# A two-layer decoder step on one core: first projection tiles, last LayerNorm and attention scores rearranged

## The chip, the cores and the metric

The kernel runs on one core of a Trainium2 chip. The core has a matrix engine (PE, with its weight loads shown apart as PEld), a vector engine (DVE), a scalar engine (ACT), a third elementwise engine (POOL), and a queue engine (SP) that mostly issues DMAs. The metric is the device time of one execution in microseconds (us), as the median of the runs; a profiled execution also has a span, from its first to its last instruction.

## The reference

One step of a trunk with two layers over 256 prompt positions, 16 learned meta tokens ahead of them, and 8 samples of 8 tokens: 336 token columns of width 2048, all in fp32.

```
layer 0 (HGRN2):  h = x @ w_in  (2048 x 8192), split into q, f, i, g
                  gated linear recurrence per head (16 heads of 128 x 128 state), RMS norm, * silu(g)
                  y = o @ w_out;  x = LayerNorm(alpha * x + y)
layer 1 (GQA):    h = x @ w_in  (2048 x 4608), split into q (32 heads of 64), k, v (4 kv heads of 64), g
                  s = (q . k) / 8 inside a window of 128;  sink softmax;  o = p @ v;  o * silu(g)
                  y = o @ w_out;  x = LayerNorm(alpha * x + y) -> y_prompt, y_sample
```

Outputs are also the new recurrent states and the new key and value caches. Prompt queries see keys of the previous and of their own block; sample queries see 128 cached keys and the 8 new ones.

## The kernel before, in words

Tokens stand along the columns (the free axis), features along the 128 partitions: `xh[k]`, `xl[k]` for k = 0..15 hold the input as a high and a low part in fp32r (a rounded float32 which PE takes in one pass, where a plain fp32 matmul shows two records). `trans_x(k)` (L297) makes them: four PE transposes (two prompt blocks, 64 sample rows, 16 meta rows) into one PSUM tile, one ACT copy for the high part and one DVE subtract for the low part.

A **projection tile** is 128 output features against all token columns. `Stream.run` (L185) walks a list `seq` of pairs (tile, kc), kc being a quarter of the 2048 contraction rows; a pair is four steps, one per k, and a step is three matmuls (L212 low weight x high input, L213 high x low, L214 high x high). Weights come by DMA (`raw`, L140, 14 pairs ahead), ACT rounds them (`conv_hi`, L150) and DVE subtracts (`conv`, L161). With `kouter` several tiles go through the quarters in step. After each step `st.step()` lets up to two side chains emit their next piece; a chain's `yield n` is n steps. So the order in each engine's queue is fixed while the program is built, and each engine takes its queue in order. PSUM tiles come from three pools: `pj` (3), `lv` (2), `mm` (3).

**The start** (L750-775): the first tile of f, of q and of i go in step and g0 follows alone; SP issues f0's first weights and then the input. The first four `trans_x` stand ahead of or at the first step, the other twelve in the chain `prologue` (L357), one every few steps. Seven warm-up matmuls (L314) come first of all.

**Attention** (L1018-1150): `prompt_chain(j)` takes a q tile of two heads on 64 rows each. The keys `kzh`, `kzl` have two column groups per kv head with zeros in the other head's rows, so that one matmul over 128 rows gives both heads' scores: three matmuls of 2x144 columns and three of 2x256. `sample_chain(q, u)` does likewise in plain fp32 with `kzs` and `knz`: one matmul of 128 columns and four of 256 on column quarters. `zeros()` writes the zeros.

**The end**: for each output tile j `epi_y(j)` (L1208) adds the residual, transposes (L1227), takes `bn_stats` and multiplies by the LayerNorm gain `yg`. `open_y()` (L1193), which allocates the buffers and loads `yg`, is called when the first output tile is finished. After the last tile `stats()` merges sixteen statistics, makes 1/std on POOL and a small matrix; `final_norm()` (L1303) makes the nine remaining 128x512 correction tiles on PE, adds each to the scaled value on DVE (L1319) and sends it out from SP.

Of the kernel before, what the change touches and what calls it, by code (L numbers as in the profile page):

```python
# [110 lines left out]
class Stream:  # L111
# [77 lines left out]
    def run(self):  # L189
        e = self.e  # L190
        nc = e.nc
        while self.i < len(self.seq):
            t, kc = self.seq[self.i]
            if t.get("before"):
                t["before"](kc)
            self.raw(self.i + e.DR)
            self.conv_hi(min(self.i + e.DC + 1, self.nc + 2))
            if "ps" not in t:
                t["ps"] = e.pj.tile([P, 512], F32, tag="pj", name=f"pj_{t['name']}")
                t["done"] = 0  # L200
            n0, n = t["t0"], t["n"]
            ps = t["ps"][:, :n]
            while ("hl", kc) not in t:
                self.conv(self.nc + 1)
            hi, lo = t.pop(("hl", kc))
            for kk in range(KC):
                k = kc * KC + kk
                xh = t["xh"][k][:, n0:n0 + n]
                xl = t["xl"][k][:, n0:n0 + n]
                t["done"] += 1  # L210
                first, last = t["done"] == 1, t["done"] == KT
                nc.tensor.matmul(ps, lo[:, kk, :], xh, start=first, stop=False)  # L212
                nc.tensor.matmul(ps, hi[:, kk, :], xl, start=False, stop=False)  # L213
                nc.tensor.matmul(ps, hi[:, kk, :], xh, start=False, stop=last)  # L214
# [12 lines left out]
def hybrid_trunk(tc, x_prompt, x_sample, state_hgrn, cache_k, cache_v, meta, w_in0, lb_logits, norm_w, w_out0,  # L227
# [7 lines left out]
    with es:  # L235
# [45 lines left out]
        wst = xes.enter_context(tc.tile_pool(name="wst", bufs=8, side="right"))  # L281
# [15 lines left out]
        def trans_x(k):  # L297
            t = xc[k]
            ps = pm(f"xT{k}")
            nc.tensor.transpose(ps[:, 16:144], t[:, 0, :], ident)  # L300
            nc.tensor.transpose(ps[:, 144:272], t[:, 1, :], ident)
            nc.tensor.transpose(ps[:, 272:336], t[0:64, 2, :], ident[0:64, 0:64])
            nc.tensor.transpose(ps[:, 0:16], t[64:80, 2, :], ident[64:80, 64:80])
            split(xh[k][:, 0:T], xl[k][:, 0:T], ps[:, :T])

        warm = ct("warm", [P, 1])
        nc.scalar.activation(warm, ones[:, 0:1], AF.Exp)
# [5 lines left out]
        for _ in range(7):  # L313
            nc.tensor.matmul(pw[:, 0:128], ones, ones, start=True, stop=True)  # L314
# [436 lines left out]
        first = [tiles[nm, 0] for nm in "fqi"]  # L751
# [4 lines left out]
        st.add([tiles["g", 0]] + [tiles[nm, h] for h in range(1, H) for nm in "fqig"])  # L756
        st.raw(1)
        load_x(0, 2)
        load_x(2, 2)
        st.raw(2)  # L760
        load_x(4, 4)
        st.raw(3)
        st.raw(6)
        load_x(8, 4)
        st.raw(8)
        load_x(12, 4)
        st.conv(1)
        for k in range(2):
            trans_x(k)
        started = []  # L770

        def before(kc):
            if not started:
                started.append(1)
                for k in range(2, KC):
                    trans_x(k)
                st.spawn(prologue())
# [107 lines left out]
        def open_l1():  # L885
# [7 lines left out]
            zero = L["oT"][:, 0, 0:NP]  # L893
            nc.vector.memset(zero, 0.0)
# [6 lines left out]
            for q in range(4):  # L901
                for nm in ("kzh", "kzl"):
                    t = ap1.tile([P, 2, NP], F32R, tag=f"{nm}{q}", name=f"{nm}{q}")
                    L[nm, q] = t
                t = ap1.tile([P, 2, NS], F32, tag=f"knz{q}", name=f"knz{q}")
                nc.gpsimd.memset(t, 0.0)
                L["knz", q] = t
                L["qs", q] = ap1.tile([P, 8, 4, 8], F32, tag=f"qs{q}", name=f"qs{q}")
            for q in range(2):
                t = ap1.tile([P, 4, 2, P], F32, tag=f"kzs{q}", name=f"kzs{q}")  # L910
                nc.gpsimd.memset(t, 0.0)
                L["kzs", q] = t

            def zeros():
                yield 20
                for q in range(4):
                    for nm in ("kzh", "kzl"):
                        nc.scalar.copy(L[nm, q][0:64, 1, :], zero[0:64, :])
                        nc.scalar.copy(L[nm, q][64:128, 0, :], zero[64:128, :])
                        yield 4  # L920
            st.spawn(zeros())

        def epi_k(i):
            def epi(ps):
# [8 lines left out]
                def chain():  # L933
# [8 lines left out]
                    def spread(src, u, half):  # L942
                        q, r = 2 * i + u, slice(64 * half, 64 * half + 64)
                        split(L["kzh", q][r, half, :], L["kzl", q][r, half, :], src[r, 0:NP])
                        nc.gpsimd.tensor_copy(L["knz", q][r, half, :], src[r, NP:T])
# [77 lines left out]
        def prompt_chain(j, pq):  # L1023
# [11 lines left out]
            pa = lv.tile([P, 512], F32, tag="lv", name=f"sa{j}")  # L1035
            pb = lv.tile([P, 512], F32, tag="lv", name=f"sb{j}")
# [8 lines left out]
            for c, (ps, n, m0, o) in enumerate(((pa, 144, 8, 0), (pb, 256, 152, 144))):  # L1045
                nc.vector.scalar_tensor_tensor(sm[:, :, o:o + n], ps[:, 0:2 * n].rearrange("p (h k) -> p h k", h=2),
                                               0.125, cst[:, m0:m0 + n].unsqueeze(1).to_broadcast([P, 2, n]),
                                               op0=ALU.mult, op1=ALU.add)
# [34 lines left out]
        def sample_chain(q, u):  # L1083
# [13 lines left out]
            for half in range(2):  # L1097
                r = slice(64 * half, 64 * half + 64)
                nc.scalar.copy(L["kzs", u][r, :, half, :], pt[r, :].rearrange("p (b k) -> p b k", b=4))
# [4 lines left out]
            ps = lv.tile([P, 512], F32, tag="lv", name=f"ss{q}_{u}")  # L1104
            nc.tensor.matmul(ps[:, 256:384], qs[:, 4 * u:4 * u + 4].rearrange("p b j t -> p (b j t)"), knz,
                             start=True, stop=True, skip_group_check=True)
            for i in range(4):
                b = 4 * u + i
                nc.tensor.matmul(ps[32 * i:32 * i + 32, 0:256], qs[:, b], L["kzs", u][:, i], start=True, stop=True,
                                 tile_position=(0, 32 * i), skip_group_check=True)  # L1110
# [3 lines left out]
            for n, m0, o, src in ((128, 408, 0, 0), (64, 536 + 64 * u, 128, 256)):  # L1114
                nc.vector.scalar_tensor_tensor(
                    sm[:, :, o:o + n], ps[:, src:src + 2 * n].rearrange("p (h k) -> p h k", h=2), 0.125,
                    cst[:, m0:m0 + n].unsqueeze(1).to_broadcast([P, 2, n]), op0=ALU.mult, op1=ALU.add)
# [74 lines left out]

        def open_y():  # L1193
            while L["ngate"] < KT:
                st.step()
# [4 lines left out]
            for nm, shape, dt in (("z", [P, 2, D], F32), ("zs", [P, D // 2], F32), ("bn", [P, 3, KT, 6], F32),  # L1200
# [3 lines left out]
            nc.sync.dma_start(Y["g"], ln_g[1:2, :].to_broadcast([P, D]))  # L1204
# [3 lines left out]
        def epi_y(j):  # L1208
            def epi(ps):
                if j == 0:  # L1210
                    open_y()

                def chain():
# [15 lines left out]
                    for b in range(3):  # L1229
                        nc.vector.bn_stats(Y["bn"][:, b, j, :], pt[:, 128 * b:128 * b + 128])  # L1230
# [41 lines left out]
        def stats():  # L1272
            M, S = Y["M"], Y["S"]
            mv = Y["p2"].tile([P, 3, 2], F32, tag="mv", name="mv", bufs=1)
            for b in range(3):
                nc.vector.bn_aggr(mv[:, b, :], Y["bn"][:, b].rearrange("p c s -> p (c s)"))
# [26 lines left out]
        def final_norm():  # L1303
# [3 lines left out]
            todo = [(0, 1), (0, 2), (2, 0), (1, 0), (1, 1), (2, 1), (0, 3), (1, 2), (1, 3)]  # L1307
            pools = [(e.pj, "pj"), (e.pj, "pj"), (lv, "lv"), (lv, "lv"), (mm, "mm"), (e.pj, "pj"), (mm, "mm"),
                     (mm, "mm"), (e.pj, "pj")]
            R = []  # L1310
            for i, (b, c) in enumerate(todo):
# [3 lines left out]
                                 start=True, stop=True, tile_position=(32 * b, 0))  # L1315
            for i, (b, c) in enumerate(todo):
                cs = slice(512 * c, 512 * c + 512)
                zz = Y["z"][:, b, cs] if b < 2 else Y["zs"][:, cs]
                nc.vector.scalar_tensor_tensor(zz, zz, rstd[:, b:b + 1], R[i], op0=ALU.mult, op1=ALU.add)  # L1319
                if b < 2:  # L1320
                    nc.sync.dma_start(y_prompt[0, 128 * b:128 * b + 128, cs], zz)
# [14 lines left out]
        def before_y(kc):  # L1336
            while not gated:
                st.step()
            if "n" not in Y:
                Y["n"] = 0  # L1340
                Y["p1"] = yes.enter_context(tc.tile_pool(name="y1", bufs=4))
                st.spawn(residuals())
            for t in yt:
# [43 lines left out]
```

## Time and profile before

| what | value |
|---|---|
| median of 3 runs | 1191.69 us (1191.45 to 1192.14) |
| profiled execution: own time / span | 1193.07 us / 1191.3 us |
| PE, PEld busy | 1170.4 us (98%), 1125.5 us (94%) |
| DVE, ACT, POOL busy | 792.3, 609.9, 236.8 us (67%, 51%, 20%) |
| DMA | 171.47 MB, mean 144 GB/s |
| granted PE clock over the span | 0.991 |

The span is the time from the first to the last instruction of that execution; its own time is what the run reports for the same execution, 1.77 us more. A PE record begins when the matmul starts and ends when its result is out, so that the records of a dense stream overlap: the distance between two starts is the price of a matmul there, not its duration.

### The profile page before, as it was taken

The numbers are of one execution on the slowest core, as the hardware profiler recorded it, in microseconds if no ns is written. First come the engines' busy times: TensorE is split into PE (matmuls) and PEld (weight loads), VectorE is DVE, ScalarE is ACT, GpSimd is POOL, SyncE is SP. The second block draws the span as 40 slices with busy tenths as digits, with TensorE's granted clock in tenths as the row PEclk, the third lists the DMA queues.
The fourth block names the chain that finished last, engine by engine and source line by source line (L and its number), as shares of the span: only waits on it lengthen the run. The fifth ranks groups of instructions, "written<-read, shape, count | busy, mean of one in ns | idle before, by whom it ended". The sixth has DMA issues, their size and how long they took to land.

```text
span 1191.3 us, 26295 instructions
## 1 busy us (share of the span) xinstructions
PE 1170.4 (98%) x10163; PEld 1125.5 (94%) x10163; DVE 792.3 (67%) x2049; ACT 609.9 (51%) x1779; POOL 236.8 (20%) x350
## 2 busy tenths in 40 slices
PE   9999999999999999999999999999999999999995
PEld 7999999999999999999999999988888899999994
DVE  3765666565666565566578777678777767777675
ACT  4655545545555545555444446666656655553340
POOL 3022212212212212212224332000000011144420
PEclk8999999999999999999999999999999999999997
DMA  9545655445655545655455555634244345555532
GB/s 260 145 128 159 178 146 145 138 134 160 180 145 146 138 133 161 179 145 151 136 146 145 143 146 166 180 103 129 74 116 117 89 126 162 151 151 178 144 93 89
DMA packets 328462, 171.47 MB, mean 144 GB/s; under 512 B 19085, under 2 KB 325613, under 8 KB 328167
## 3 DMA queue, kind: packets, MB, share of 16 engines
q1 hardware_dynamic: 327792, 168.82, 50.2%
q8 instruction: 80, 1.31, 0.5%
q0 software_dynamic: 544, 0.97, 0.2%
q14 instruction: 46, 0.37, 0.1%
HBM read 156.97 MB, written 14.42 MB: 144 GB/s over the span
## 4 chain that ended last, share of the span: by engine, by line
PE 92%; issue 3%; DVE 2%; DMA 1%; ACT 1%; POOL 1%; SPq 0%; POOLq 0%; DVEq 0%; ACTq 0%
PE pj_q L212 7%; PE pj_g L212 7%; PE pj_g L213 7%; PE pj_g L214 6%; PE pj_q L213 6%; PE pj_q L214 6%; PE pj_f L212 4%; PE pj_i L212 3%; PE pj_i L214 3%; PE pj_i L213 3%; PE pj_f L214 3%; PE pj_f L213 3%; PE pj_z L214 3%; PE pj_z L213 3%; PE pj_z L212 3%
## 5 line engine op out<-in xcount | busy, mean ns | idle before, releaser
L212 PE MATMUL pj_q<-xh,wlo_q 128*128 128x336 f32 (+1 forms) x512 | 166.6, 325 | 0.0
L212 PE MATMUL pj_g<-xh,wlo_g 128*128 128x336 f32 (+1 forms) x512 | 162.9, 318 | 0.0
L213 PE MATMUL pj_q<-xl,whi_q 128*128 128x336 f32 (+1 forms) x512 | 161.2, 315 | 0.0
L214 PE MATMUL pj_q<-xh,whi_q 128*128 128x336 f32 (+1 forms) x512 | 160.9, 314 | 0.0
L213 PE MATMUL pj_g<-xl,whi_g 128*128 128x336 f32 (+1 forms) x512 | 160.6, 314 | 0.0
L214 PE MATMUL pj_g<-xh,whi_g 128*128 128x336 f32 (+1 forms) x512 | 160.4, 313 | 0.0
L212 PEld LDWEIGHTS pj_q<-xh,wlo_q 128*128 128x128 f32 x512 | 97.1, 190 | 5.8 <-issue 4.7
L212 PEld LDWEIGHTS pj_g<-xh,wlo_g 128*128 128x128 f32 x512 | 96.6, 189 | 1.5 <-issue 1.3
L213 PEld LDWEIGHTS pj_q<-xl,whi_q 128*128 128x128 f32 x512 | 97.3, 190 | 0.5
L214 PEld LDWEIGHTS pj_q<-xh,whi_q 128*128 128x128 f32 x512 | 97.1, 190 | 0.0
L213 PEld LDWEIGHTS pj_g<-xl,whi_g 128*128 128x128 f32 x512 | 96.8, 189 | 0.1
L214 PEld LDWEIGHTS pj_g<-xh,whi_g 128*128 128x128 f32 x512 | 96.6, 189 | 0.0
L169 DVE TENSOR_TENSOR wlo_g<-raw_g,whi_g 128x512 fp32r<-128x512 f32 x128 | 90.4, 743 | 0.6 <-ACT whi_g L158 0.6
L169 DVE TENSOR_TENSOR wlo_q<-raw_q,whi_q 128x512 fp32r<-128x512 f32 x128 | 85.1, 684 | 5.3 <-ACT whi_q L158 5.3
L212 PE MATMUL pj_f<-xh,wlo_f 128*128 128x336 f32 x256 | 83.7, 327 | 0.0
L213 PE MATMUL pj_f<-xl,whi_f 128*128 128x336 f32 x256 | 81.5, 318 | 0.0
L214 PE MATMUL pj_f<-xh,whi_f 128*128 128x336 f32 x256 | 81.5, 318 | 0.0
L212 PE MATMUL pj_i<-xh,wlo_i 128*128 128x336 f32 x256 | 81.4, 318 | 0.0
L212 PE MATMUL pj_z<-oh,wlo_z 128*128 128x336 f32 x256 | 81.3, 317 | 0.0
L214 PE MATMUL pj_z<-oh,whi_z 128*128 128x336 f32 x256 | 81.1, 317 | 0.0
L213 PE MATMUL pj_z<-ol,whi_z 128*128 128x336 f32 x256 | 81.0, 316 | 0.0
L213 PE MATMUL pj_i<-xl,whi_i 128*128 128x336 f32 x256 | 80.9, 316 | 0.0
(401 smaller groups left out, 3161.2 us busy)
## 6 DMA issues: line engine op xcount, KB each, us to landing
raw_g<-in_hgrn_w_in_dram SPq DMA_DIRECT2D x32, 512.0 KB
raw_z<-in_hgrn_w_out_dram SPq DMA_DIRECT2D x32, 512.0 KB
raw_q<-in_swa_w_in_dram SPq DMA_DIRECT2D x32, 512.0 KB
raw_g<-in_swa_w_in_dram SPq DMA_DIRECT2D x32, 512.0 KB
raw_y<-in_swa_w_out_dram SPq DMA_DIRECT2D x32, 512.0 KB
raw_f<-in_hgrn_w_in_dram SPq DMA_DIRECT2D x30, 512.0 KB
raw_q<-in_hgrn_w_in_dram SPq DMA_DIRECT2D x30, 512.0 KB
raw_i<-in_hgrn_w_in_dram SPq DMA_DIRECT2D x30, 512.0 KB
```

The costliest lines, as they stand in the source:

```text
L169: e.nc.vector.tensor_tensor(lo, t.pop(("raw", kc)), hi.bitcast(F32), op=ALU.subtract)
L212: nc.tensor.matmul(ps, lo[:, kk, :], xh, start=first, stop=False)
L213: nc.tensor.matmul(ps, hi[:, kk, :], xl, start=False, stop=False)
L214: nc.tensor.matmul(ps, hi[:, kk, :], xh, start=False, stop=last)
```

## The change

Five things are edited.

1. The tiles f0, q0, i0 and g0 go in step (g0 in a bank of the `lv` pool). The first weight DMA is issued by ACT, ahead of ACT's table load; SP begins with the input. Weights and input are asked for in another order, `wst` has nine buffers, and there are eight warm-up matmuls.
2. `trans_x` makes three transposes: sample and meta rows are one block of 80 rows. The parts are now written by two ACT copies and two DVE subtracts, since prompt and sample columns stand in another order in PSUM. Three `trans_x` come ahead of the stream, the fourth after its first step.
3. Prompt scores: each head has its own 64 rows and its own PSUM tile, and twelve matmuls of 144 or 256 columns on row halves (`tile_position=(64 * h, 0)`) take the place of six. The zero halves, and what writes them, are gone. Sample scores: sixteen matmuls on row halves and column quarters take the place of five.
4. `open_y` runs in a chain of its own as soon as all gates are done, and `yg` is loaded in four pieces.
5. Last LayerNorm: fifteen of the sixteen statistics are merged one tile early; the epsilon is folded into them. Of the nine corrections the three for the second prompt block (columns 512 on) are scaled on ACT, copied from PSUM by ACT, added on POOL and sent from ACT's queue; DVE keeps six.

```
 def trans_x(k):
-            nc.tensor.transpose(ps[:, 16:144], t[:, 0, :], ident)
-            nc.tensor.transpose(ps[:, 144:272], t[:, 1, :], ident)
-            nc.tensor.transpose(ps[:, 272:336], t[0:64, 2, :], ident[0:64, 0:64])
-            nc.tensor.transpose(ps[:, 0:16], t[64:80, 2, :], ident[64:80, 64:80])
-            split(xh[k][:, 0:T], xl[k][:, 0:T], ps[:, :T])
+            nc.tensor.transpose(ps[:, 80:208], t[:, 0, :], ident)
+            nc.tensor.transpose(ps[:, 208:336], t[:, 1, :], ident)
+            nc.tensor.transpose(ps[:, 0:80], t[0:80, 2, :], ident[0:80, 0:80])
+            nc.scalar.copy(xh[k][:, 0:NP], ps[:, NS:T])
+            nc.scalar.copy(xh[k][:, NP:T], ps[:, 0:NS])
+            nc.vector.tensor_tensor(xl[k][:, 0:NP], ps[:, NS:T], xh[k][:, 0:NP].bitcast(F32), op=ALU.subtract)
...
 def prologue():
-            yield 2
+            trans_x(3)
+            yield 8
             for k in range(KC, KT):
                 trans_x(k)
-                yield 3
+                yield 2 if k < 2 * KC - 1 else 4
...
-        first = [tiles[nm, 0] for nm in "fqi"]
+        first = [tiles[nm, 0] for nm in "fqig"]
+        first[3]["bank"] = lv, "lv"
...
-        st.raw(1)
+        st.raw(1, nc.scalar)
+        nc.scalar.activation(warm, ones[:, 0:1], AF.Exp)
         load_x(0, 2)
         load_x(2, 2)
-        st.raw(2)
+        st.raw(4)
         load_x(4, 4)
-        st.raw(3)
-        st.raw(6)
+        st.raw(8)
         load_x(8, 4)
-        st.raw(8)
+        st.raw(10)
         load_x(12, 4)
         st.conv(1)
-        for k in range(2):
+        for k in range(3):
             trans_x(k)
...
 def prompt_chain(j, pq):
-            for ps, n, t0, k0, k1 in ((pa, 288, 0, 0, 144), (pb, 512, 128, 16, 272)):
-                o = ps[:, 0:n]
-                nc.tensor.matmul(o, ql[:, t0:t0 + 128], kh[:, :, k0:k1], start=True, stop=False)
-                nc.tensor.matmul(o, qh[:, t0:t0 + 128], kl[:, :, k0:k1], start=False, stop=False)
-                nc.tensor.matmul(o, qh[:, t0:t0 + 128], kh[:, :, k0:k1], start=False, stop=True)
+            for o, n, t0, k0 in ((0, 144, 0, 0), (144, 256, 128, 16)):
+                for i, (a, b) in enumerate(((ql, kh), (qh, kl), (qh, kh))):
+                    for h in range(2):
+                        nc.tensor.matmul(pa[h][:, o:o + n], a[hs[h], t0:t0 + 128], b[hs[h], k0:k0 + n], start=i == 0,
+                                         stop=i == 2, tile_position=(64 * h, 0), skip_group_check=True)
...
 def sample_chain(q, u):
+            for o, n in ((0, 128), (128, 64)):
+                for i in range(4):
+                    for h in range(2):
+                        r = slice(64 * h, 64 * h + 64)
+                        nc.tensor.matmul(ps[h][32 * i:32 * i + 32, o:o + n], qs[r, 4 * u + i],
+                                         knz[r, :] if o else L["kzs", u][r, i], start=True, stop=True,
+                                         tile_position=(64 * h, 32 * i), skip_group_check=True)
...
+        def opening():
+            while L["ngate"] < KT:
+                yield 1
+            open_y()
...
 def stats():
-                nc.vector.bn_aggr(mv[:, b, :], Y["bn"][:, b].rearrange("p c s -> p (c s)"))
+                nc.vector.bn_aggr(mv[:, b, :], Y["ag"][:, b, :])
-            nc.vector.tensor_scalar(rstd, mv[:, :, 1], LN_EPS, None, op0=ALU.add)
-            nc.gpsimd.tensor_tensor(rstd, rstd, mhalf[:, 0:3], op=ALU.pow)
+            nc.gpsimd.tensor_tensor(rstd, mv[:, :, 1], mhalf[:, 0:3], op=ALU.pow)
...
 def final_norm():
-            todo = [(0, 1), (0, 2), (2, 0), (1, 0), (1, 1), (2, 1), (0, 3), (1, 2), (1, 3)]
+            todo = [(0, 1), (1, 1), (2, 0), (0, 2), (1, 2), (2, 1), (0, 3), (1, 3), (1, 0)]
+            for c in range(1, 4):
+                nc.scalar.activation(part(1, c), part(1, c), AF.Copy, scale=rstd[:, 1:2])
...
+                if b == 1 and c:
+                    r = Y["g"][:, 512 * c:512 * c + 512]
+                    nc.scalar.copy(r, R[i])
+                    nc.gpsimd.tensor_tensor(zz, zz, r, op=ALU.add)
+                    late.append((c, zz))
+                    continue
...
+            for c, zz in late:
+                nc.scalar.dma_start(y_prompt[0, 128:256, 512 * c:512 * c + 512], zz)
```

The order of the queues moves at three places that matter below. First, ACT at the start, before (`xh_78` to `xh_81` are the high parts for k = 0 to 3, `whi_q_0` the rounded first weight quarter of q0):

```order
L158 CAST whi_f_0_223<-raw_f_0_187 128x512
L264 CAST xh_78<-xT_227 128x336
L264 CAST xh_79<-xT_234 128x336
L264 CAST xh_80<-xT_243 128x336
L264 CAST xh_81<-xT_250 128x336
L158 CAST whi_q_0_267<-raw_q_0_197 128x512
L158 CAST whi_i_0_269<-raw_i_0_203 128x512
```

And with the change:

```order
L158 CAST whi_f_0_228<-raw_f_0_187 128x512
L305 CAST xh_78<-xT_232 128x272
L306 CAST xh_78<-xT_232 128x64
L305 CAST xh_79<-xT_240 128x272
L306 CAST xh_79<-xT_240 128x64
L305 CAST xh_80<-xT_248 128x272
L306 CAST xh_80<-xT_248 128x64
L158 CAST whi_q_0_266<-raw_q_0_198 128x512
L158 CAST whi_i_0_268<-raw_i_0_200 128x512
L305 CAST xh_81<-xT_274 128x272
L306 CAST xh_81<-xT_274 128x64
```

The input's fourth part now stands behind the first weights of q0 and i0. Second, PE at the scores of the first q tile, before:

```order
L1039 MATMUL sa_10566<-kzh_10074,ql_10547 128x288
L1040 MATMUL sa_10566<-kzl_10075,qh_10546 128x288
L1041 MATMUL sa_10566<-kzh_10074,qh_10546 128x288
L1039 MATMUL sb_10567<-kzh_10074,ql_10547 128x512
L1040 MATMUL sb_10567<-kzl_10075,qh_10546 128x512
L1041 MATMUL sb_10567<-kzh_10074,qh_10546 128x512
```

And with the change (`sa` is now the first head's tile, `sb` the second's):

```order
L1030 MATMUL sa_10564<-kzh_10094,ql_10545 128x144
L1030 MATMUL sb_10565<-kzh_10094,ql_10545 128x144
L1030 MATMUL sa_10564<-kzl_10095,qh_10544 128x144
L1030 MATMUL sb_10565<-kzl_10095,qh_10544 128x144
L1030 MATMUL sa_10564<-kzh_10094,qh_10544 128x144
L1030 MATMUL sb_10565<-kzh_10094,qh_10544 128x144
L1030 MATMUL sa_10564<-kzh_10094,ql_10545 128x256
L1030 MATMUL sb_10565<-kzh_10094,ql_10545 128x256
```

The row halves alternate, and each instruction has half the columns that both heads had together. Third, SP where the gain `yg` is asked for, before (each `raw_y` is half a contraction of an output tile's weights):

```order
L147 DMA raw_y_0_14337<-in_swa_w_out_dram 128x8x128
L147 DMA raw_y_2_14387<-in_swa_w_out_dram 128x8x128
L147 DMA raw_y_0_14431<-in_swa_w_out_dram 128x8x128
L147 DMA raw_y_2_14470<-in_swa_w_out_dram 128x8x128
L147 DMA raw_y_0_14509<-in_swa_w_out_dram 128x8x128
L147 DMA raw_y_2_14547<-in_swa_w_out_dram 128x8x128
L1204 DMA yg<-in_ln_g_dram 128x2048
L1205 DMA yb<-in_ln_b_dram 128x512
```

And with the change:

```order
L147 DMA raw_y_0_14535<-in_swa_w_out_dram 128x8x128
L147 DMA raw_y_2_14585<-in_swa_w_out_dram 128x8x128
L147 DMA raw_y_0_14629<-in_swa_w_out_dram 128x8x128
L1198 DMA yg<-in_ln_g_dram 128x512 x4
L1199 DMA yb<-in_ln_b_dram 128x512
```

Both pieces begin at the fourth output tile's first half, so the gain is asked for three weight loads earlier.

More of the change, by code (lines that the diff above doesn't have):

```diff
@@ L902, in open_l1 @@
                 for nm in ("kzh", "kzl"):
[L903 to L907, printed above, removed]
+                    L[nm, q] = ap1.tile([P, NP], F32R, tag=f"{nm}{q}", name=f"{nm}{q}")
+                L["knz", q] = ap1.tile([P, NS], F32, tag=f"knz{q}", name=f"knz{q}")
                 L["qs", q] = ap1.tile([P, 8, 4, 8], F32, tag=f"qs{q}", name=f"qs{q}")
             for q in range(2):
[L910 to L921, printed above, removed]
+                L["kzs", q] = ap1.tile([P, 4, P], F32, tag=f"kzs{q}", name=f"kzs{q}")
         def epi_k(i):
@@ L1096, in sample_chain @@
             yield 1
-            for half in range(2):
-                r = slice(64 * half, 64 * half + 64)
-                nc.scalar.copy(L["kzs", u][r, :, half, :], pt[r, :].rearrange("p (b k) -> p b k", b=4))
+            nc.scalar.copy(L["kzs", u].rearrange("p b k -> p (b k)"), pt)
             yield 3
@@ L1103, in sample_chain @@
             yield 7 + 8 * u
[L1104 to L1110, printed above, removed]
+            ps = [lv.tile([P, 512], F32, tag="lv", name=f"ss{c}{q}_{u}") for c in "ab"]
+            for o, n in ((0, 128), (128, 64)):
+                for i in range(4):
+                    for h in range(2):
+                        r = slice(64 * h, 64 * h + 64)
+                        nc.tensor.matmul(ps[h][32 * i:32 * i + 32, o:o + n], qs[r, 4 * u + i],
+                                         knz[r, :] if o else L["kzs", u][r, i], start=True, stop=True,
+                                         tile_position=(64 * h, 32 * i), skip_group_check=True)
             yield 1
```

72 lines of the change are left out of this document (39 added, 33 removed).

## The prediction

> **What bounds the kernel now.** I read the page first, then the waits of PE, then the order of time where the change works.
>
> ```profile
> PE 1170.4 (98%) x10163; PEld 1125.5 (94%) x10163; DVE 792.3 (67%) x2049; ACT 609.9 (51%) x1779; POOL 236.8 (20%) x350
> ```
> ```profile
> PE yt L1227 <- DVE z L1217: 1.7, 2, 1.2
> PE xT L300 <- DMA xin<-in_x_prompt_dram: 0.9, 1, 0.9
> ```
>
> PE works without a break; of the 20.9 us left, most is the last 17 us, after the last projection. So an edit is worth what it takes out of PE's stream, at the pitch of starts and not by the durations, plus what it does to the start, where PE runs slowly, and to the end, where PE is done. Other engines count only where PE waits for them. The clock at the start (columns: window, busy times, granted clock, DMA share, GB/s):
>
> ```profile
> 8.00:10.00 2.00, 2.00 (x9) 1.91 (x10) 1.02 (x2) 0.50 (x2) 0.00 (x0) 0.60 1.08 293
> ...
> 18.00:20.00 2.00, 2.00 (x12) 1.73 (x11) 0.58 (x1) 0.66 (x2) 2.00 (x5) 0.84 1.08 327
> ```
>
> Means of 0.60 and 0.84 between half and full put the half clock from 8.4 to 18.6 us.
>
> **Input transposes and the start.** PE, in order of time, at half clock, at full clock around one group of four transposes, and around three output transposes:
>
> ```profile
> 9.15 0.48 PE L212 MATMUL pj_f<-xh,wlo_f 128*128 128x336 f32 x1
> ...
> 9.99 0.48 PE L212 MATMUL pj_f<-xh,wlo_f 128*128 128x336 f32 x1
> ...
> 29.84 0.32 PE L214 MATMUL pj_i<-xh,whi_i 128*128 128x336 f32 x1
> 29.99 0.27 PE L300 MATMUL xT<-ident,xin 128*128 128x128 f32 x1
> ...
> 30.93 0.32 PE L213 MATMUL pj_f<-xl,whi_f 128*128 128x336 f32 x1
> ...
> 32.01 0.32 PE L214 MATMUL pj_f<-xh,whi_f 128*128 128x336 f32 x1
> ```
> ```profile
> 1167.96 0.31 PE L214 MATMUL pj_y<-ph,whi_y 128*128 128x320 f32 x1
> 1168.12 0.49 PE L1227 MATMUL yt<-ident,z 128*128 128x128 f32 x3
> ...
> 1168.59 0.31 PE L213 MATMUL pj_y<-pl,whi_y 128*128 128x320 f32 x1
> ```
>
> From 30.93 to 32.01 are seven starts: 0.154 us each, 0.46 a step, and 0.84 a step at half clock. From L214 to the second start behind the group are 1.09 us where 0.31 would do, so four transposes cost 0.78; three over all rows cost 0.63 - 0.29 = 0.34. The new third block has 80 rows, so it needs more than the lower 64: I take 0.34 for each of the twelve later groups, a gain of 0.44 each.
>
> The start needs a time line, since ACT's new order adds a wait: `xh_81`, without which step 4 cannot run, stands behind the rounding of i0's first weights, and DVE's `xl_97` and q0's subtract behind that.
>
> ```profile
> 4.64 0.42 SPq L147 DMA_DIRECT2D raw_q<-in_hgrn_w_in_dram  x1
> ...
> 6.80 0.42 SPq L147 DMA_DIRECT2D raw_i<-in_hgrn_w_in_dram  x1
> ```
> ```profile
> 10.08 0.62 ACT L158 CAST whi_q<-raw_q 128x512 fp32r<-128x512 f32 x1 [1.28 <-DMA raw_q<-in_hgrn_w_in_dram]
> 13.34 0.62 ACT L158 CAST whi_i<-raw_i 128x512 fp32r<-128x512 f32 x1 [2.64 <-DMA raw_i<-in_hgrn_w_in_dram]
> ```
> ```profile
> 7.36 0.23 PE L303 MATMUL xT<-ident,xin 16*128 16x16 f32 x1
> ```
>
> The third input part was there by 7.36; its DMAs move up by one SP slot (about 0.5 us, f0 going to ACT's queue), so the stream can start at 7.0 instead of 8.25. Steps 1 to 3 and one transpose group end at 9.1, the last of them at half clock. i0 is now asked for at about 4.6, q0's old place; such loads took 5.4 and 6.5 us, so it lands at 10.0 to 11.1, or 8.5 if the 512 KB of input now behind it was what slowed q0. I take 10.2; cast 0.62 and the two copies (336 columns) about 0.45: step 4 starts at 11.3, a new wait of 2.2 us. Then nothing is late: by the queue's order the next input lands near 13 and is used near 16. Before, dense work from 13.1 brought the clock back at 18.6, 5.5 us later; the same from 11.3 gives 16.8. The Trainium skill ("TensorE: Matmul & The Clock Gate", Part 1) says that full clock follows a busy window of about 3.4 us out of free-running ones; the low stretch of 10.2 us is three of them, which agrees, and by it the clock comes back at 15.2 or at 18.6, worth 0.8 us more or less than my value.
>
> Left at 11.3 are 61 steps (28.1 us), twelve groups (4.1) and one transpose (0.1); 5.5 us at half clock do 3.0 of it. The four tiles end at 16.8 + 29.3 = 46.1. Before they ended at 52.5 (the row of 52.33 below is g0's last matmul). **Gain 6.4**; bounds 4.6 (i0 at 11.1, clock at 18.6, stream half a us late) and 8.4 (no wait, 15.2). The extra small copies on ACT and DVE hide under engines half idle there.
>
> **Prompt scores**, sixteen times. One insertion before; loads of 128 columns with nothing to hide them; a first load after a change of tile shape; column quarters:
>
> ```profile
> 760.27 0.32 PE L214 MATMUL pj_q<-xh,whi_q 128*128 128x322 f32 x1
> ...
> 761.52 0.31 PE L212 MATMUL pj_q<-xh,wlo_q 128*128 128x322 f32 x1
> 761.67 0.31 PE L213 MATMUL pj_q<-xl,whi_q 128*128 128x322 f32 x1
> ```
> ```profile
> 720.42 0.66 PEld L846 LDWEIGHTS ln_var<-ones,m 128*128 128x128 f32 x6
> 721.01 0.19 PEld L212 LDWEIGHTS pj_k<-xh,wlo_k 128*128 128x128 f32 x1
> ```
> ```profile
> 773.97 0.19 PEld L212 LDWEIGHTS pj_q<-xh,wlo_q 128*128 128x128 f32 x1 [0.17 <-issue]
> ```
> ```profile
> 52.33 0.32 PE L214 MATMUL pj_g<-xh,whi_g 128*128 128x336 f32 x1
> 52.58 0.40 PE L516 MATMUL lv_a<-qp,kr 128*32 128x32 f32 x24
> ...
> 53.61 0.42 PE L212 MATMUL pj_f<-xh,wlo_f 128*128 128x336 f32 x1
> ```
> ```profile
> 1179.49 1.22 PE L1314 MATMUL R<-ygb,SL 5*128 5x512 f32 x6 [0.35 <-ACT SL L1298]
> ```
>
> Before: 1.40 - 2 x 0.15 = 1.10 us. After: entering another tile shape costs 0.25 - 0.15 = 0.10 (52.33 to 52.58), leaving it 0.17 (773.97) and another 0.10 at the next load (798.07 to 798.32 below, less 0.15): 0.37. That row halves run side by side is shown by the last row, on row groups: six matmuls of 512 columns at half clock, 0.28 x 512/336 = 0.43 each in a row, take 1.22 and not 2.6. At 0.154/336 us a column, two halves side by side stream in 3 x (0.066 + 0.117) = 0.55. A load costs 0.59/6 = 0.10, more than 144 columns: 3 x 0.10 + 3 x 0.117 = 0.65 if halves load side by side too. I take that: 1.02, **gain 0.08 x 16 = 1.3**. Bounds: streaming alone, 0.92, gain 3.0; all loads and streams in a row, 6 x 0.10 + 6 x 0.117 + 0.37 = 1.67, loss 9.1. The skill's Part 3 of the same page has packed matmuls start about 4 ns apart; by it the sum is that of streaming alone.
>
> **Sample scores**, eight times:
>
> ```profile
> 797.03 0.31 PE L214 MATMUL pj_q<-xh,whi_q 128*128 128x322 f32 x1
> 797.18 0.38 PE L1105 MATMUL ss<-knz,qs 128*128 128x128 f32 x2
> 797.50 0.64 PE L1109 MATMUL ss<-kzs,qs 128*32 128x256 f32 x8
> 798.07 0.41 PE L212 MATMUL pj_q<-xh,wlo_q 128*128 128x322 f32 x1
> 798.32 0.31 PE L213 MATMUL pj_q<-xl,whi_q 128*128 128x322 f32 x1
> ```
>
> Before 1.29 - 0.30 = 0.99. Sixteen fp32 matmuls are 32 records; the 96 records of L516 take 1.03, so 0.34, plus 0.37: 0.71. **Gain 0.28 x 8 = 2.2**; bounds -1.5 (32 loads of 32 columns in a row at a quarter of 0.10) and 2.6. The score chains now need both `lv` tiles; DVE reads each with one instruction and frees them no later than before.
>
> **The gain's load.** The 1.2 us wait of L1227 follows from this row:
>
> ```profile
> 1077.05 0.42 DVE L1234 TENSOR_TENSOR yz<-yt,yg 128x256 f32<-128x256 f32 x1 [1.79 <-DMA yg<-in_ln_g_dram]
> ```
>
> It is now asked for three weight loads (about 3.5 us each) earlier. **Gain 1.2** (0 to 1.3).
>
> **The end:**
>
> ```profile
> 1175.60 1.46 DVE L1276 BATCH_NORM_AGGREGATE mv<-ybn 128x2 f32<-128x96 f32 x3
> ...
> 1186.00 1.53 SPq L1321 DMA_DIRECT2D out_dram<-yz  x3
> ```
> ```profile
> 1182.00:1189.50 7.50, 0.00 (x0) 0.00 (x0) 4.33 (x7) 0.00 (x0) 0.00 (x0) 0.50 0.93 309
> ```
> ```profile
> L645 POOL TENSOR_TENSOR vm<-Vs,cst 112x512 fp32r<-112x512 f32 x32 | 33.0, 1052 | 236.4 <-ACT Vs L640 236.4
> ...
> L1187 POOL TENSOR_TENSOR res<-res,rbc 128x320 f32<-128x320 f32 x16 | 17.9, 1121 | 23.1 <-DVE res L1185 23.1
> ```
>
> Merging 9 numbers instead of 96 saves up to 1.46; I take 1.2 with the dropped addition, and all that follows moves up. Three DVE additions less are worth 2.0, but the DMA engines are 93% busy until 1189.5, so I count 0.8 of that. POOL's adds cost 1.05 to 1.8 each by the two rows; starting near 1180.7 they end at 1184 to 1186, ahead of the 1187.5 at which SP issued last. **Gain 2.0** (1.0 to 3.2).
>
> **Sum.** 6.4 + 1.3 + 2.2 + 1.2 + 2.0 = 13.1: 1193.07 - 13.1 = 1180.0 for the profiled execution (its span 1191.3 to 1178.2). The median stands 1.4 below that execution: **1178.6 us**.
>
> **Rivals.**
> A: a further load is late at the start, by as much as i0 came behind q0 (13.34 - 10.08 = 3.3 us), at full clock, since the weights of four tiles now share the DMAs with the input: a start worth 3.1, 1181.9. For it: DMA shares near 1 in both rows of the clock; against: by the queue's order all else is asked for well ahead of its use.
> B: the 144-column matmuls run at plain fp32's rate, as no fp32r matmul under 320 columns (288 in the scores) is in the trace: L1105 gives 0.22 for 128 columns, so 0.25; 3 x (0.25 + 0.117) + 0.37 = 1.47, 5.9 lost where I gain 1.3: 1185.8.
> C: loads and streams of the halves go in a row, the 1.67 above: 1189.0. The skill's same page (LDWEIGHTS) says that a load's time goes by columns and not by rows, which speaks for twice the load time; the six matmuls in 1.22 speak against a full queue.
> D, the other side: matmuls on row halves lose fp32r's one pass altogether: 3 x (0.25 + 0.44) + 0.37 = 2.44, 21.4 lost: 1201.3. It decides once an insertion costs over 1.10 + 11.8/16 = 1.84. For it: no fp32r matmul on 64 rows is shown; against: the row of R, also fp32r on a row group.
>
> **Chances.** Forecast 62% (its own range 1174 to 1182), A 12, B 9, C 10, D 7. What can be told from no change here is 0.2%, 2.4 us: C lies at its edge and is halved. Faster 88%, same 5%, slower 7%. The range runs from 1173.5 to 1189.
>
> **What would show it.** Four tiles done by 46 to 48 us; a wait of ACT for `raw_i` ahead of `xh`; groups of transposes costing 0.34; score insertions of about 1.0 and 0.7; no wait of L1227 near 1080; from last projection to the end 15.5 us instead of 17.5. An insertion above 1.5, or a fourth tile done after 50, would make it wrong.

## The result, and the profile after

| | before | after |
|---|---|---|
| median | 1191.91 us (1191.45 to 1193.34, 4 runs) | 1180.70 us (1178.98 to 1182.20, 4 runs) |
| ratio, 95% interval | | 0.9903 (0.9886 to 0.9921) |
| profiled execution: own time / span | 1193.07 / 1191.3 us | 1182.2 / 1180.4 us |

The changed kernel takes about 1% less time, and no change lies well outside the interval. The forecast of 1178.6 us lies 2.1 us below the median; the time is inside the forecast's own range (1174 to 1182). PE is as full as before; its busy time fell by 10.9 us, as much as the span. The page of the changed kernel, then the longest waits of its PE (total, times, longest):

```profile
PE 1159.5 (98%) x10421; PEld 1117.4 (95%) x10421; DVE 789.0 (67%) x2080; ACT 602.8 (51%) x1777; POOL 236.5 (20%) x348
```
```profile
PE pS L1298 <- DVE yS L1296: 2.6, 1, 2.6
PE pss L688 <- DVE osc L732: 1.6, 1, 1.6
PE pj_f L213 <- ACT xh L306: 1.4, 1, 1.4
...
PE yt L1221 <- DVE z L1211: 0.9, 2, 0.5
```

The third line is new: step 4 of f0 waits for `xh_81`. Of the fourth, 0.51 us stands at the last tile and stood there before too. The other 0.37 us is no longer a wait for `yg`: DVE's `z` stands behind a part of the next weights, which waits for ACT's cast of them, and that for their load.

```profile
1068.78 0.69 DVE L169 TENSOR_TENSOR wlo_y<-raw_y,whi_y 128x512 fp32r<-128x512 f32 x1 [0.93 <-ACT whi_y L158]
```

To see where the time went I set side by side the rows at which a stage starts: the first output tile of layer 0 (z), layer 1 (k), the output projection (y), and the last projection. Before:

```profile
585.88 0.32 PE L212 MATMUL pj_z<-oh,wlo_z 128*128 128x336 f32 x1
713.28 0.32 PE L212 MATMUL pj_k<-xh,wlo_k 128*128 128x338 f32 x1
1054.68 0.31 PE L212 MATMUL pj_y<-ph,wlo_y 128*128 128x320 f32 x1
1173.58 0.31 PE L214 MATMUL pj_y<-ph,whi_y 128*128 128x320 f32 x1
```
After:
```profile
578.81 0.32 PE L213 MATMUL pj_z<-oh,wlo_z 128*128 128x336 f32 x1
707.03 0.32 PE L213 MATMUL pj_k<-xh,wlo_k 128*128 128x338 f32 x1
1045.69 0.31 PE L213 MATMUL pj_y<-ph,wlo_y 128*128 128x320 f32 x1
1163.67 0.31 PE L215 MATMUL pj_y<-ph,whi_y 128*128 128x320 f32 x1
```

| stage | before | after | gain | forecast |
|---|---|---|---|---|
| to z: start and heads | 585.88 | 578.81 | 7.07 | 6.4 |
| z to k | 127.40 | 128.22 | -0.82 | 0 |
| k to y: attention | 341.40 | 338.66 | 2.74 | 3.5 (1.3 + 2.2) |
| y to last projection | 118.90 | 117.98 | 0.92 | 1.2 |
| from there to the end of the span | 17.7 | 16.7 | 1.0 | 2.0 |
| sum | | | 10.9 | 13.1 |

Between the first tiles and z both kernels do the same work, so z serves as the mark for the start: it is behind the same work in both orders, which the first tiles themselves are not. All gains are against one traced execution of the kernel before, 1.2 us above the median of its four runs, and its start may differ between executions as the new one does.

### The profile page after: what moved, and what is told of

Its sections match the earlier page's. It is cut to its first block, busy times and chain, and to the rows that moved or that the text cites. A ratio compares the mean times of both kernels' runs of the same rounds, so it can differ in the third digit from the quotient of the medians.

```text
span 1180.4 us, 26871 instructions
## 1 busy us (share of the span) xinstructions
PE 1159.5 (98%) x10421; PEld 1117.4 (95%) x10421; DVE 789.0 (67%) x2080; ACT 602.8 (51%) x1777; POOL 236.5 (20%) x348
## 3 DMA queue, kind: packets, MB, share of 16 engines
q10 hardware_dynamic: 960, 1.05, 0.3%
## 4 chain that ended last, share of the span: by engine, by line
PE 94%; DMA 2%; POOL 1%; DVE 1%; ACT 1%; issue 0%; SPq 0%; POOLq 0%; DVEq 0%; ACTq 0%
PE pj_q L213 7%; PE pj_g L213 7%; PE pj_g L214 7%; PE pj_g L215 7%; PE pj_q L214 6%; PE pj_q L215 6%; PE pj_f L213 3%; PE pj_i L213 3%; PE pj_i L215 3%; PE pj_i L214 3%; PE pj_f L214 3%; PE pj_f L215 3%; PE pj_z L215 3%; PE pj_z L214 3%; PE pj_z L213 3%; PE pj_y L215 3%
## 5 line engine op out<-in xcount | busy, mean ns | idle before, releaser
L215 PE MATMUL pj_i<-xh,whi_i 128*128 128x336 f32 x256 | 81.0, 316 | 0.0
```

## The experiments

Each ran beside runs of the kernel before on its own chip; the ratio is to those. Effects below 1 us are read from the stage marks of the profiled execution, since repeated runs of one kernel spread by up to 5 us.

**The changed kernel again** (e5).

> The changed kernel itself once more, for the variants to be compared with on one chip. The start should differ from execution to execution: in one profiled execution step 4 waited 1.44 us and the clock then stood at half for 3.41 us; with the same start code in the run with the old prompt scores neither was there, and the four tiles were done 1.6 us earlier. If that is chance (when i's first weights land, and where the clock's windows fall), this execution may show either, and the times spread by some 2 us: 1179 to 1182.

Measured: 1180.75 us, ratio 0.9913 (0.9899 to 0.9927). Five more executions have the same start code (this one and e4, e7, e8, e11 below). z begins at 578.81, 578.48, 576.97, 577.38, 578.89 and 576.95 in the six: a start worth 7.0 to 8.9 us, 8.0 in the mean. What differs is waits and the clock. In the first execution, around step 4 and in the clock:

```profile
9.51 0.62 ACT L158 CAST whi_i<-raw_i 128x512 fp32r<-128x512 f32 x1 [1.18 <-DMA raw_i<-in_hgrn_w_in_dram]
...
10.58 0.42 PE L213 MATMUL pj_f<-xh,wlo_f 128*128 128x336 f32 x1 [1.44 <-ACT xh L306]
```
```profile
12.00:14.00 2.00, 2.00 (x9) 2.00 (x9) 1.02 (x2) 0.36 (x1) 0.00 (x0) 0.60 1.21 275
14.00:16.00 2.00, 2.00 (x11) 1.94 (x10) 0.59 (x1) 1.00 (x2) 0.00 (x0) 0.55 1.11 273
```

Means of 0.60 and 0.55 put 1.6 and 1.8 us at half clock there: one stretch of 3.4 us. In e5 i0's weights came sooner, the wait at step 4 was 0.84 us and the clock stayed full, but a second wait of the same kind came near 30 us: the cast of g0's third weights waits for its load, and the copies of an input block stand behind it. In e4 and e8 there was no wait at step 4, but the first three steps ran at half clock, with starts 0.28 us apart until 10.4 and 10.7 us: the slower steps took up the time of the wait.

```profile
9.97 0.42 PE L213 MATMUL pj_f<-xh,wlo_f 128*128 128x336 f32 x1 [0.84 <-ACT xh L306]
...
30.22 0.42 PE L213 MATMUL pj_f<-xh,wlo_f 128*128 128x336 f32 x1 [0.64 <-ACT xh L306]
```
```profile
29.15 0.62 ACT L158 CAST whi_g<-raw_g 128x512 fp32r<-128x512 f32 x1 [2.00 <-DMA raw_g<-in_hgrn_w_in_dram]
```

**Transposes alone, and order alone** (e1, e6). e1 puts the new `trans_x` into the kernel before; e6 takes it out of the changed kernel.

```
 e1, in before / e6 the reverse, in the changed kernel
-    four transposes, split(xh[k][:, 0:T], xl[k][:, 0:T], ps[:, :T])
+    three transposes, two ACT copies, two DVE subtracts
```

> The kernel before with one part of the change alone: three input transposes and two copies each, the first tiles still in the old order. My steps count 0.44 us for each of twelve later groups, so 5.3 of the start's 7.1 us would come from here: 1191.9 - 5.3 = 1186.6. Rival: PE at the start is paced by loads that land late (DMA share near 1 until 21 us), so a shorter stream only waits longer and most of the 7.1 comes from the order: a gain of 2 or less, 1190 or more, with new waits of PE for DMA before 25 us.

> The changed kernel with four transposes and one split per input block, as before; the order of the start stays changed. By my steps the twelve later groups cost 0.44 us more each, 5.3 in all: about 1186.0, so the new order alone is worth only some 2 us of the start. By the run with the transposes alone (4.1 us less at the end of the first tiles): 1184.8. Rival: the order is worth most, transposes little: 1182.5 or less.

Measured: e1 1188.03 us, ratio 0.998 (0.997 to 0.9991), z at 581.57, 4.3 us ahead of before. By the times it gained only 3.0 on its own chip (1191.01 before), where 5.3 was expected; the traced execution is the slowest of its twelve, at 1191.43, and lost 2.6 again between y and the last projection. e6 1184.86 us, ratio 0.9947 (0.9934 to 0.9961), z at 582.27, 3.6 ahead; beside e5, timed on the same chip, the transposes are worth 4.1. By z the two are 4.3 and 3.6, and add up to 7.9, near the 8.0 of the six executions. My steps had 5.3 for the transposes and so 1.1 for the order. The price of one group was right; the changed kernel has, from a third matmul to the second start behind three transposes,

```profile
21.52 0.32 PE L215 MATMUL pj_f<-xh,whi_f 128*128 128x336 f32 x1
...
21.92 0.40 PE L213 MATMUL pj_f<-xh,wlo_f 128*128 128x336 f32 x1
22.16 0.31 PE L214 MATMUL pj_f<-xl,whi_f 128*128 128x336 f32 x1
```

0.64 - 0.31 = 0.33 us. e6 shows no wait of PE after 5.4 us in the first tiles, and stood at half clock from 7.6 to 11.0 us. Its like among the six is e4, at half clock until 10.4 and without a wait at step 4 or near 30 us: z, which comes ahead of e4's old scores, is 582.27 and 576.97 there, 5.3 apart, the whole forecast. In the mean of the six, 4.1 to 4.4 arrives; that the rest goes into waits for loads fits this pair, but it is one pair of executions. In e1 a half-clock stretch followed such a wait, of 1.27 us (means of 0.77 and 0.59 below), and another its wait for `yg`, 2.46 us long there (mean 0.50):

```profile
20.16 0.42 PE L212 MATMUL pj_f<-xh,wlo_f 128*128 128x336 f32 x1 [1.27 <-ACT xh L304]
```
```profile
20.00:22.00 2.00, 1.65 (x7) 1.36 (x8) 1.86 (x6) 1.03 (x4) 0.52 (x1) 0.77 1.20 256
22.00:25.00 3.00, 3.00 (x15) 2.94 (x15) 0.97 (x3) 1.17 (x4) 0.00 (x0) 0.59 1.15 339
```
```profile
1076.11 0.91 PE L1229 MATMUL yt<-ident,z 128*128 128x128 f32 x3 [2.46 <-DVE z L1219]
```
```profile
1076.00:1078.00 2.00, 1.89 (x8) 1.89 (x9) 1.20 (x7) 1.51 (x3) 1.28 (x2) 0.50 0.86 239
```

**What takes the clock to half** (e3, e12). e3 fills the hole ahead of step 4, e12 makes it longer.

```
 e3, between steps 3 and 4 of f0
+    for _ in range(6): nc.tensor.matmul(pf[:, 0:128], ones, ones, start=True, stop=True)
 e12, in prologue()
+    for _ in range(7): nc.scalar.copy(xh[15][:, 0:256]..., xc[0][:, 0:2, :])
     trans_x(3)
```

> The changed kernel with six matmuls on a constant, results unused, between steps 3 and 4 of f0, where PE waits 1.44 us. The wait itself stays. If the hole is what takes the clock to half for 3.41 us, the stretch is gone and the four tiles end 1.7 us earlier: 1179.0. Rival: the half clock comes from something else (the count of busy windows since the start, as the 10.2 us before): the stretch stays and the time is 1180.7.

> The changed kernel with seven more copies on ACT (256 columns each, into a part of xh that is written again later) ahead of xh_81, so the hole in PE's stream ahead of step 4 grows from 0.6 to 1.4 us to about 2.6 to 3.4 us. If a hole of more than about half a window of 3.41 us takes the clock to half for the next window, a half-clock stretch of 3.41 us begins at 11 to 14 us whatever the windows' place, and the four tiles end at 46 to 47.5 us. Rival: the clock at the start does not hang on holes: no such stretch, and they end at 45.4 to 46, since part of the hole is covered by loads that are late anyway.

Measured: e3 1181.15 us, ratio 0.9915 (0.9901 to 0.9929), no half clock, z at 577.24. That settles nothing by itself, since e5, e7 and e11 had none after the stream's start either, with holes of 0.84, 1.05 and 0.50 us left in. e12 shows that a hole can do it: 1183.76 us, ratio 0.9938 (0.9919 to 0.9958), z at 580.38, and behind a hole of 3.47 us a stretch of 0.18 x 2 + 0.50 x 2 + 0.17 x 2, doubled, 3.4 us:

```profile
12.66 0.42 PE L213 MATMUL pj_f<-xh,wlo_f 128*128 128x336 f32 x1 [3.47 <-ACT xh L306]
```
```profile
12.00:14.00 2.00, 1.15 (x4) 0.82 (x4) 1.36 (x4) 1.13 (x4) 0.00 (x0) 0.82 1.15 276
14.00:16.00 2.00, 2.00 (x9) 2.00 (x9) 1.53 (x3) 0.86 (x2) 0.00 (x0) 0.50 1.20 299
16.00:18.00 2.00, 2.00 (x13) 1.98 (x13) 0.18 (x1) 1.00 (x2) 0.00 (x0) 0.83 1.09 306
```

So a hole can cost 1.7 us more than itself. Its length alone does not decide: PE waits 1.56 or 1.57 us for `osc` between 584 and 595 us in all fourteen executions, longer than the 1.44 at step 4, and the clock stays full behind it. In the changed kernel:

```profile
588.01 0.47 PE L688 MATMUL pss<-vm,Ks 112*128 112x512 f32 x1 [1.57 <-DVE osc L732]
```
```profile
587.00:589.00 2.00, 0.99 (x7) 0.95 (x8) 1.66 (x4) 0.00 (x0) 0.27 (x1) 1.00 0.62 183
589.00:591.00 2.00, 2.00 (x14) 1.85 (x12) 1.46 (x6) 1.01 (x3) 0.00 (x0) 1.00 0.06 18
```

That the 1.44 us hole took the clock to half in the first execution, where the stretch began 1.8 us behind it, is thus possible but not shown.

**Can the new wait be taken away?** (e2, e9)

```
 e2                                        e9, in prologue()
-    for k in range(3):                   -  at k == 5:  mkf, cst loads
+    for k in range(4):                   +  at k == 12: gate on xh[12], then mkf, cst loads
         trans_x(k)
```

> The changed kernel, the fourth input block transposed ahead of the stream instead of after its first step, so that ACT makes xh_81 ahead of the casts of q0 and i0. The 1.44 us wait of step 4 goes; three transposes (0.33) come ahead: about 1.2 us, 1179.5. If that hole in the stream is also what takes the clock to half from 12.38 to 15.8 us, another 1.7 (half of 3.41) is there, of which about 1.0 can be used, since xh_82 stands on ACT behind the cast of i's second weights (landed at 16.5) and is ready about 2.2 us before its use: 1178.5, and no half-clock stretch. Rival: the next load is late by as much, and nothing is gained: 1180.7.

> The changed kernel with the loads of the masks and the constants (0.78 MB, asked for at 20 to 21 us, used after 36) behind the last input transposes. If the first tiles are now paced by the DMAs (share near 1 until 30 us, casts of weights waiting for them), 0.78 MB at some 290 GB/s bring the third weights of g0 about 2.7 us earlier, and the wait for the input block that stands on ACT behind their cast (0.6 and 1.0 us near 30 us in two executions) is gone: first tiles done by 43.9 us, 1179.8. Rival: the wait comes from the order of ACT alone, or the loads are late for another reason: no change, 45.3 and 1180.8.

Measured: e2 1180.08 us, ratio 0.991 (0.9895 to 0.9925), z at 577.64. The wait at step 4 is gone and the clock is full throughout, and yet it is no better than the unchanged starts: the input then comes late,

```profile
13.75 0.26 PE L304 MATMUL xT<-ident,xin 80*128 80x80 f32 x1 [0.77 <-DMA xin<-in_meta_tokens_dram]
```

which is its rival. e9: 1179.66 us, ratio 0.9902 (0.9887 to 0.9917), z at 576.62, the earliest of all, and no wait near 30 us. The direction fits loads that pace the start, but four of the six unchanged executions had no such wait either, and the intervals of e5 and e9 overlap: not shown.

**Prompt scores** (e4, e8, e11).

```
 e4   the six matmuls over 128 rows, the zero halves and their writing, as before
 e8   for o, n, t0, k0 in ((0, 256, 0, 0), (144, 256, 128, 16)):      # 144 -> 256
 e11  after the 144-column matmuls:  yield 1
```

> The changed kernel with the prompt scores as before (zero halves, six matmuls over 128 rows, and the copies that write the zeros). By my forecast's term 1.3 us is lost: 1182.0. By the two traces, in which an insertion went from 1.38 to 1.35 us, 0.4 to 0.5: 1181.2. If the row halves in fact cost time elsewhere (DVE reads both banks in one instruction, so the softmax starts later, and a wait for it grew from 0.14 to 0.51 us), it is faster: 1180.3.

> The changed kernel with the first score matmuls made 256 columns wide instead of 144 (columns 144 to 255 are written over afterwards, so results are the same). If a pair of 144 columns is held by its two weight loads (0.11 us from start to start), 256 columns cost 0.01 to 0.05 more each: an insertion grows by 0.05 to 0.15 us. If it is held by streaming, as a pure streaming sum has it, it grows by 3 x 112 columns, 0.15 us, from a lower level. If both halves load in turn, nothing changes at all.

> The changed kernel with the prompt scores in two insertions, the 144-column matmuls one step ahead of the 256-column ones, so PE goes to row halves and back twice as often. By my forecast's 0.37 us for entry and exit, sixteen more cost 5.9 us between the first q tile and the first gate tile (179.2 becomes 185.1). By the starts inside one insertion (0.09 in, 0.09 out, 0.11 at the next load) 0.29 each, 4.6. If the cost lies in the loads of the halves and not in the switch: 0 to 1.

Measured: e4 1180.08 us, ratio 0.9909 (0.9894 to 0.9925); from k to y 338.61 us against 338.66: the new prompt scores are worth nothing. e8, timed once, 1182.01 us: an insertion grows by 0.013 us (median of eleven, 1.384 to 1.397), so 112 more columns are nearly free. e11, timed once, 1186.21 us: the insertions of 1.384 become two of 0.98 and 1.04, 0.31 us of ordinary stream in each, so 0.33 us more (medians of insertions between steps of the stream), and from first q tile to first gate tile it is 184.4 instead of 179.2. That total also holds 1.4 us more of other waits of PE than the changed kernel has there (2.1 against 0.6); without them it gives 3.7 / 16 = 0.23 us for going there and back. One insertion of the changed kernel:

```profile
754.02 0.32 PE L215 MATMUL pj_q<-xh,whi_q 128*128 128x322 f32 x1
754.26 0.34 PE L1030 MATMUL sa<-kzh,ql 64*128 64x144 f32 x1
754.27 0.33 PE L1030 MATMUL sb<-kzh,ql 64*128 64x144 f32 x1
754.43 0.27 PE L1030 MATMUL sa<-kzl,qh 64*128 64x144 f32 x1
...
754.66 0.33 PE L1030 MATMUL sa<-kzh,ql 64*128 64x256 f32 x1
...
755.15 0.42 PE L213 MATMUL pj_q<-xh,wlo_q 128*128 128x322 f32 x1
755.41 0.31 PE L214 MATMUL pj_q<-xl,whi_q 128*128 128x322 f32 x1
```

The halves do run side by side (754.26 and 754.27), but pairs of 144 columns start 0.11 us apart, as their loads do:

```profile
754.37 0.19 PEld L1030 LDWEIGHTS sa<-kzl,qh 64*128 64x128 f32 x1
754.37 0.19 PEld L1030 LDWEIGHTS sb<-kzl,qh 64*128 64x128 f32 x1
754.48 0.19 PEld L1030 LDWEIGHTS sa<-kzh,qh 64*128 64x128 f32 x1
```

That is the sum I took, loads before streaming, and e8 rules out streaming alone, with which 0.15 us more were due. By the Trainium skill ("TensorE: Matmul & The Clock Gate", Part 3) packed matmuls start some 4 ns apart; within a pair the trace agrees (3 to 4 ns). It is the step from one pair to the next, 0.11 us, that decides the sum here.

**The corrections at the end** (e7).

```
 in final_norm(): todo, pools and the loop as before; no ACT scaling, no POOL adds, no ACT queue
```

> The changed kernel with the nine corrections at the end as before, all added on DVE and sent from SP; the early merge of fifteen statistics stays. By my forecast 0.8 us is lost: from last projection to the end 17.6 us instead of 16.8. If the output DMAs end the kernel in both, nothing is lost: 16.8. If the copies on ACT and the adds on POOL in fact delay the last output, it is faster: 16.4.

Measured: 1181.21 us, ratio 0.9916 (0.9904 to 0.9929); from last projection to the end 16.9 us. The executions with the new corrections have 16.6 to 17.2: no difference. The output DMAs end the kernel in both. DMA share and GB/s are the last two columns; the changed kernel, then e7:

```profile
1174.00:1176.00 2.00, 0.00 (x0) 0.00 (x0) 0.00 (x0) 0.00 (x0) 0.30 (x1) 0.50 0.99 268
1176.00:1178.00 2.00, 0.00 (x0) 0.00 (x0) 0.00 (x0) 0.00 (x0) 0.00 (x0) 0.50 1.00 378
```
```profile
1174.00:1176.00 2.00, 0.00 (x0) 0.00 (x0) 0.00 (x0) 0.00 (x0) 0.00 (x0) 0.50 0.97 372
```

**All of it together** (e10): e2 and e9, and the state of each head asked for one tile earlier.

```
 def epi_g(h):
-    s0 = hp.tile(...); nc.sync.dma_start(s0, state_hgrn[0, :, h]...)
 def epi_i(h):
+    s0 = hp.tile(...); nc.sync.dma_start(s0, state_hgrn[0, :, h]...)
```

> The changed kernel with the fourth input block ahead, late masks and constants, and each head's state asked for when i is finished instead of g, one tile earlier. First tiles done near 42.5 us (no wait at step 4, none at 30 us) and the stretch from the first output tile of layer 0 to layer 1 at 127.4 us as before the change instead of 127.8 to 128.2, since the last head's state is there in time: 1178.0. Rival: the earlier request waits in SP's queue for its buffer and holds up the weights behind it: new waits of PE for weights in the heads, 1181 or more.

Measured: 1179.75 us, ratio 0.9903 (0.9887 to 0.992); span 1177.3. z to k is 127.39 us, as before the change, where the eleven other executions with four tiles in step have 127.45 to 128.22. In the changed kernel the last head's state landed 9.4 us after it was asked for at 581.92, when z's first tile was already running:

```profile
591.28 0.64 PE L711 MATMUL po<-s,sq 128*32 128x128 f32 x16 [0.15 <-DMA s<-in_state_hgrn_dram]
591.30 1.90 POOL L699 TENSOR_TENSOR ns<-s,fs 128x1024 f32<-128x1024 f32 x1 [4.03 <-DMA s<-in_state_hgrn_dram]
```

Over the executions with the old request the stretch follows this load: POOL's row starts 11.4 us behind z in the kernel before (z to k 127.40), 11.5 in e6 (127.45), 12.0 to 12.1 in e4, e5, e11 and e12 (127.76 to 127.79), and 12.5 in the changed kernel (128.22). So the loss of 0.82 is this load, though PE's own waits there are only 0.15 and 0.36 us. Why it takes 9.4 us, against 8.3 before, stays open. e10 also lost the wait at step 4 and the one near 30 us, as expected, but PE then waited 0.46 and 0.60 us for the input near 13 us. By the times it cannot be told from the changed kernel: the ratios of e10 and e5 overlap.

## Why the prediction was right, and where its steps were not

The sum came out 2.2 us too large in the profiled execution. Five terms are behind it, and they went both ways; the mechanisms of the start, the sample scores, the gain's load and the early merge were as forecast, but that the total is so near is in part luck.

- **Start, 6.4 forecast, 7.1 and, over six executions, 7.0 to 8.9 measured.** The direction and the new wait of step 4 behind i0's cast came as foretold, for the reason given; i0 landed at 8.5 to 9.5 and not at 10.2, so the wait was 0.5 to 1.4 us, or none at half clock, and not 2.2. The step that failed is the clock: I let it stand at half until 16.8, by analogy with before. It was full from 5.6 to 6.7 us on in three of the six executions and from 10.4 and 10.7 on in two; in the profiled one it was full from 5.6 us and fell to half for one stretch of 3.4 us behind the hole. So the order is worth 3.6 (e6) and not 1.1. "Then nothing is late" failed too: near 30 us a second wait of 0.6 to 1.0 us came in two of six, and the transposes gave 4.1 of 5.3. That is rival A's mechanism at a third of its price or less. The start's total came within 0.7 us by luck: the order was put 2.5 too low and the transposes about 1.2 too high.
- **Prompt scores, 1.3 forecast, 0 measured.** 1.02 us was forecast for the new insertion, 1.384 - 0.308 = 1.08 measured; and the old one was 1.08 over eleven, where I read 1.10 from one row. Sixteen times a difference of 0.08, between two sums that were off by 0.02 and 0.06, was no forecast at all. Of the parts, entry and exit are 0.23 to 0.33 (e11; 0.37 forecast), and loads and streams the other 0.75 to 0.85 (0.65). Rivals B, C and D are out: at 1.08 us an insertion lies far below their 1.47, 1.67 and 2.44.
- **Sample scores, 2.2 forecast.** An insertion went from 1.286 to 0.982 us (medians of eight), 2.4 in all; the remaining 0.3 of the stage's 2.74 is near the 0.4 us wait of `ck` for `sm` in the kernel before, which the changed one does not have.
- **The gain's load, 1.2 forecast, 0.9 measured,** and 1.5 in nine of the eleven other executions, whose stretch from y to the last projection is 117.39. The wait for `yg` is gone in all; in the profiled one, in e3 and in e9 the late weights shown above took a part of the gain. In e1, with the old opening, the stretch was 121.53.
- **The end, 2.0 forecast, 1.0 measured.** The merge did its part (the kernel before, then after):

```profile
1179.18 0.26 ACT L1298 CAST SL<-pS 96x128 fp32r<-96x128 f32 x1 [20.73 <-PE pS L1296]
```
```profile
1167.92 0.26 ACT L1300 CAST SL<-pS 96x128 fp32r<-96x128 f32 x1 [21.55 <-PE pS L1298]
```

`SL` follows the last projection's start by 4.25 us instead of 5.60, 1.35 where I took 1.2. But then I added 0.8 for the corrections, and this is the term that failed: e7 shows 0 to 0.2. Of the 1.35 too only 0.8 arrived in e7 (16.9 instead of 17.7), and the DMAs run near full there until some 2.5 us before the end. I had written their share of 93% down and still counted the term.
- **Left out:** the last head's state, 0.4 to 0.8 us lost. I asked which loads of the start would be late next, not whether any load was only just in time elsewhere; in the kernel before POOL already waited 3.0 us for it, at a place where PE did not yet follow.

## What to carry to other kernels

When PE is saved work at a stage that loads pace, only part arrives: look for the operations that stand behind a cast of late weights in the same engine's queue, since the shorter stream runs into them. Count a gain that is the difference of two nearly equal sums as zero until an insertion of each kind has been measured over all its repeats. And where the DMAs are above 90% busy up to the end, as here, do not count on faster engines: e7 shows them worth nothing here.

## What the hardware showed that was not expected

A hole in PE's dense stream can cost more than its length. Behind holes of 1.27, 1.44, 2.46 and 3.47 us the clock stood at half for one stretch of 3.4 us, 1.7 us of work; behind holes of 0.50 to 1.05 us in the first tiles, of 1.2 us for `yg` in the kernel before, and of 1.6 us for `osc` in all fourteen executions, it did not. In e6 and e8 the clock also fell to half for 3.4 us, at 7.6 and 7.3 us, where little but the transposes ahead of the stream, with holes of 0.5 and 1.0 us, lay before it. So no length of hole divides the two cases. By the Trainium skill ("TensorE: Matmul & The Clock Gate", Part 1) the window is 3.4 us long and free-running, which agrees with the stretches: in the changed kernel the clock changes at 12.38, 15.79 and again at 1169.50 us, 339 x 3.413 behind the first. A hole then falls into one window or two by chance, which would help to explain why the same start differs by 1.9 us between executions. But the window's place does not settle it either: in the changed kernel the hole of 1.44 us and that of 1.57 both lie wholly inside one such window (8.97 to 12.38, and 585.8 to 589.2). What decides stays open.

Going to row halves and back cost 0.23 to 0.33 us an insertion in these scores (e11), about two ordinary matmuls; the Trainium skill ("TensorEngine Tiling (Array Packing)", Key Properties) says that a change of mode drains the engine, and names no price.
